# Attention units of a decoder layer: by token tile of a head pair instead of by branch

## The chip, the cores and the metric

The kernel runs on one core of a Trainium2 chip. The metric is the device time of one execution in microseconds; the kernel before was run three times (median 1426.13, from 1425.64 to 1426.88). A separate, profiled execution took 1427.72 us; its trace covers a span of 1425.9 us from the first to the last instruction.

## The reference, cut to what matters

One decoder layer on 256 tokens of width 2048, all in float32. After a norm, one matrix `w_in` projects to queries, keys, values and gates of two groups of 16 heads of 64. The first 16 heads are "NSA" heads: four query heads share a key/value head, and each head mixes three branches. With 256 tokens all four blocks of 64 keys are selected and the window of 512 covers everything, so the selected and the window branch are both plain causal attention over all keys, with the same relative bias, but with keys and values of their own:

```python
s = einsum(q, k_slc) * scale + bias        # 256 x 256, causal, per head
o_slc = masked_softmax(s) @ v_slc
s = einsum(q, k_win) * scale + bias_w      # the same bias by distance
o_win = masked_softmax(s) @ v_win
o = g0 * o_cmp + g1 * o_slc + g2 * o_win   # gates per token and head
```

The third branch attends to 15 compressed blocks. The other 16 heads ("FoX") are causal attention with a forget gate. Both are normed, multiplied by `w_out` and added to the input; then come a router and 32 experts (top two), whose weights alone are some 400 MB, and a last norm.

## The kernel before, in words

The work has three stages. In the first (to about 370 us of the span) `w_in` streams through SBUF in 44 items; each item is four chunks of 12 matmuls that accumulate into PSUM. Float32 accuracy comes from splitting each operand x into hi + lo, two numbers in the faster float32r form, and adding the products hi·hi, hi·lo and lo·hi: `stream_conv` makes the two halves of a weight (ACT writes hi at L187, DVE writes lo at L188) into one of three buffers, two half items ahead. In the second stage `w_out` streams in the same way (`wo`, 386 to 460 us). The third is the experts: their weights stream through a ring of SBUF slots (`expert_load`, L960); a load is issued by SP when its slot is free and when the stage allows it (`ring["ready"]`, `ring["used"]`, both advanced as the matmuls are issued).

The order on every engine is the order of the program. Attention is woven into the streaming: after every chunk `background()` advances the pipeline `attn_pipe` by one step. Its four steps per unit are: `a` of the next unit, `b` of the unit before it, nothing, `c` of the unit before it. One unit is thus consumed per item; there are 16 units for the NSA heads and 8 for FoX.

An NSA unit (class `Unit`) is one branch `br` of a pair of heads (pair `p`, 8 pairs):

- `a` computes logits of both heads, for the token tile t=1 (tokens 128 to 255, 256 keys) and t=0 (128 keys), into one PSUM bank per head; DVE adds the bias and takes the row maximum (L573), ACT takes the exponential and its sum (L575), DVE inverts the sum, multiplies by the gate and scales (L579 to L584).
- `b` turns the probabilities round by six 128x128 transposes (L591 to L593) and copies them out of PSUM, head 0 on DVE, head 1 on ACT (L595).
- `c` multiplies with the values: four products, head 0 into rows 0 to 63 of the bank `o` and head 1 into rows 64 to 127. At the pair's second branch the compressed branch is added (`pTc`) and ACT copies the result out (L614).

The logits use the same split. `split_k` writes for each key head hi and lo, each in both halves of the partitions; `split_q` writes a head's q as hi in one half and lo in the other (`qs`). The two products of a head are

```python
(qs[:, j, h, tk], kk[:, 0, g, keys])      # 128 rows: hi and lo of q with hi of k
(qs[hp, j, h, tk], kk[hp, 1, g, keys])    # 64 rows: hi of q with lo of k
```

where `hp` is rows 0 to 63 for head 0 and rows 64 to 127 for head 1. `mm` (L114) issues all of these matmuls, so in the profile they are told apart by the names of their tiles: `s_n` logits, `t_n` transposes, `o` values (`_f` for FoX).

Of the kernel before, what the change touches and what calls it, by code (L numbers as in the profile page):

```python
# [80 lines left out]
def tile_kernel(ctx: ExitStack, tc: tile.TileContext, a: dict, out):  # L81
# [441 lines left out]
    kT, vN = {}, {}  # L523

    def split_k(tmp, kk):
        for gp in range(2):
            hp, op_ = slice(64 * gp, 64 * gp + 64), slice(64 - 64 * gp, 128 - 64 * gp)
            act.copy(kk[hp, 0, gp::2, :], tmp[hp])
            dve.tensor_tensor(kk[hp, 1, gp::2, :], tmp[hp], kk[hp, 0, gp::2, :].bitcast(F32), ALU.subtract)
            yield  # L530
            for part in range(2):
                act.copy(kk[op_, part, gp::2, :], kk[hp, part, gp::2, :].bitcast(F32))
                yield

    def post_kv(b, br):
# [4 lines left out]
        splits.append(split_k(tmp, kk))  # L540
# [3 lines left out]
        kT[br], vN[br] = kk, vt  # L544


    sq = fp.tile([P, 2, T], F32, name="sq")

    class Unit:
# [3 lines left out]
        def __init__(self, name, qk, bias, v, gmul, first, last, pair):  # L553
            self.__dict__.update(locals())

        def a(self):
# [21 lines left out]
            for h in range(2):  # L578
                dve.tensor_scalar(sm[:, h], sm[:, h], 1e-30, None, ALU.max)  # L579
                dve.reciprocal(sm[:, h], sm[:, h])  # L580
                if self.gmul is not None:
                    dve.tensor_tensor(sm[:, h], sm[:, h], self.gmul[:, h], ALU.mult)
# [3 lines left out]
        def b(self):  # L586
            self.t = []
            for h in range(2):
# [5 lines left out]
                pT = wk.tile([P, 384], F32, tag="pT", name=f"pT_{self.name}_{h}", bufs=4)  # L594
                (act.copy if h else dve.tensor_copy)(pT, tp[:, 0:384])  # L595
                self.t.append(pT)

        def c(self):
            pr = self.pair
            if self.first:  # L600
                pr["o"] = bank(f"o{pr['i']}", "o")
            oT = pr["o"]
            hp = [slice(0, 64), slice(64, 128)]
            nsa = pr["i"] < 8
            for h in range(2):
                mm(oT[hp[h], 0:T], self.v[h][0], self.t[h][:, 0:T], self.first, False)
            for h in range(2):
                mm(oT[hp[h], P:T], self.v[h][1], self.t[h][:, T:T + P], False, self.last and not nsa)
            if self.last:
                i = pr["i"]  # L610
                if nsa:
                    G, j = divmod(i, 4)
                    mm(oT[:, :T], vcbd[0][:, G, j, :], pTc[G], False, True)
                act.copy(oraw[i // 8][:, i % 8, :], oT[:, :T])  # L614
                part = i // 8
                if i % 8 == 0:
                    pool.tensor_tensor(sq[:, part, :], oraw[i // 8][:, i % 8, :], oraw[i // 8][:, i % 8, :], ALU.mult)
                else:
                    s2 = wk.tile([P, T], F32, tag="pcm", name=f"s2_{i}", bufs=1)
                    pool.tensor_tensor(s2, oraw[i // 8][:, i % 8, :], oraw[i // 8][:, i % 8, :], ALU.mult)  # L620
                    pool.tensor_tensor(sq[:, part, :], sq[:, part, :], s2, ALU.add)
# [71 lines left out]
    def post_q(b, G):  # L693
# [7 lines left out]
        for j in range(4):  # L701
# [5 lines left out]
            def bias_of(g=g, hs=hs, nxt=j % 2 == 1):  # L707
                bi = nsa_bias(g)
                if nxt:
                    nsa_bias(g + 1) if g < 3 else fox_bias(0)  # L710
                return [(bi[:, hh, P - 1::-1], bi[:, hh, T - 1::-1]) for hh in hs]

            for br in range(2):
                def qk(h, t, keys, j=j, g=g, kk=kT[br]):
                    tk, hp = slice(t * P, (t + 1) * P), slice(64 * h, 64 * h + 64)
                    return [(qs[:, j, h, tk], kk[:, 0, g, keys]), (qs[hp, j, h, tk], kk[hp, 1, g, keys])]

                units.append(Unit(f"n{p}{br}", qk, bias_of,
                                  [[vN[br][:, t, 64 * g:64 * g + 64] for t in range(2)]] * 2,
                                  gb[:, 2 * p:2 * p + 2, :, br + 1], br == 0, br == 1, pair))  # L720
# [15 lines left out]
    def post_fkv(b, G, hf):  # L736
# [5 lines left out]
        for j in range(2):  # L742
# [10 lines left out]
            def qk(h, t, keys, j=j):  # L753
# [6 lines left out]
                              None, True, True, pair))  # L760
# [728 lines left out]
```

## Time and profile before

| | |
|---|---|
| median of 3 runs | 1426.13 us |
| profiled execution | 1427.72 us, span 1425.9 us |
| TensorE busy | 1321.7 us, 93% of the span |
| DVE, ACT, POOL busy | 509.2, 315.3, 75.9 us |
| HBM read | 476.63 MB |
| attention units of the NSA heads | 125 to 278 us of the span |

A busy TensorE says that an instruction was in it, not that it streamed columns: matmuls overlap, and a gap of a tenth of a microsecond between two starts is counted as busy. What an instruction costs is therefore read here from the distance between starts on the time line, not from its duration. In a row of a time line, the number before the engine is the time from the first start to the last end of the group, and a shape such as 64*128 is rows times columns of the stationary operand.

### The profile page before, as it was taken

The page shows a single profiled execution, that of the slowest core. Times are in us where ns is not written, and L with a number is a line of the kernel's source. Part 1 is how long each engine was busy: PE and PEld are TensorE (multiplying, and loading weights), DVE is VectorE, ACT ScalarE, POOL GpSimd, SP SyncE. Part 2 cuts the span into 40 slices and gives each one's busy share as a digit, 9 for nine tenths or more (in the row PEclk, how much of TensorE's full clock was granted, in tenths as well). Part 3 has the DMA queues.
Part 4 walks back from the last instruction along what each step waited for, and adds up shares of the span by engine and source line. Part 5 has one row for each costly group of instructions (what it writes and reads, how often), then busy time and mean ns, then how long its engine had stood idle before and what let it go on. Part 6 is the DMA issues. An engine that isn't in the chain of part 4 may idle for free.

```text
span 1425.9 us, 18327 instructions
## 1 busy us (share of the span) xinstructions
PE 1321.7 (93%) x7526; PEld 771.5 (54%) x7526; DVE 509.2 (36%) x1046; ACT 315.3 (22%) x632; POOL 75.9 (5%) x94
## 2 busy tenths in 40 slices
PE   9999999999999899999998997997998899799885
PEld 8999999889787534334333432433433344243332
DVE  4656877766756304114113021220401212031022
ACT  5455555545545100100100000000000000000003
POOL 0300010131100003000000000000000000000003
PEclk9999999999999999999999999999999999999998
DMA  8654454555595999999999999999999999999994
GB/s 270 211 165 149 133 143 134 182 171 167 197 378 184 362 398 422 399 421 421 421 421 421 421 420 421 421 420 421 421 420 421 421 421 421 421 420 421 421 405 162
DMA packets 116698, 480.04 MB, mean 337 GB/s; under 512 B 14368, under 2 KB 40832, under 8 KB 68352
## 3 DMA queue, kind: packets, MB, share of 16 engines
q1 hardware_dynamic: 112240, 474.53, 84.5%
q10 hardware_dynamic: 4368, 4.27, 0.9%
q8 instruction: 61, 1.00, 0.3%
q14 instruction: 29, 0.24, 0.1%
HBM read 476.63 MB, written 2.14 MB: 336 GB/s over the span
## 4 chain that ended last, share of the span: by engine, by line
PE 56%; DMA 37%; DVE 4%; ACT 2%; issue 1%; SPq 0%; ACTq 0%; POOL 0%; DVEq 0%; POOLq 0%
DMA e_u<-in_expert_w_up_dram 17%; DMA e_d<-in_expert_w_down_dram 17%; PE bu L114 12%; PE fkv_ps L114 6%; PE wo L114 6%; PE bg L114 4%; PE by L114 4%; PE bo L114 3%; PE q_ps L114 3%; PE fq_ps L114 3%; PE bx L114 3%; DMA e_g<-in_expert_w_gate_dram 3%; PE kcv_ps L114 2%; PE o L114 2%; PE kvw_ps L114 2%; PE kvs_ps L114 2%
## 5 line engine op out<-in xcount | busy, mean ns | idle before, releaser
L114 PE MATMUL by<-e_d,hids 128*64 128x512 f32 (+2 forms) x1072 | 234.0, 576 | 32.5 <-DMA e_d<-in_expert_w_down_dram 31.8
L114 PE MATMUL bu<-e_u,xg 128*64 128x512 f32 x1024 | 243.9, 597 | 9.7 <-DMA e_u<-in_expert_w_up_dram 9.6
L114 PE MATMUL bg<-e_g,xg 128*64 128x512 f32 x1024 | 234.8, 596 | 12.9 <-DMA e_g<-in_expert_w_gate_dram 12.9
L1273 DVE TENSOR_TENSOR ys<-by,ys 128x512 fp32r<-128x512 f32 x60 | 40.0, 687 | 454.1 <-ACT ys L1272 452.8
L114 PEld LDWEIGHTS by<-e_d,hids 128*64 128x64 f32 x1072 | 77.4, 137 | 181.8 <-issue 122.1
L114 PEld LDWEIGHTS bg<-e_g,xg 128*64 128x64 f32 x1024 | 81.7, 137 | 143.2 <-issue 107.0
L114 PEld LDWEIGHTS bu<-e_u,xg 128*64 128x64 f32 x1024 | 75.6, 136 | 148.3 <-issue 121.5
L1287 DVE TENSOR_TENSOR y<-y,bo 128x512 f32<-128x512 f32 x112 | 72.0, 684 | 152.7 <-PE bo L114 152.7
L1272 ACT CAST ys<-by 128x512 fp32r<-128x512 f32 x60 | 35.2, 586 | 311.8 <-PE by L114 197.2
L114 PE MATMUL bo<-ys,scT 128*128 128x512 f32 x240 | 73.5, 426 | 13.4 <-DVE y L1287 5.8
L114 PE MATMUL wo<-cv_wo,ohi 128*128 128x512 f32 x256 | 80.6, 396 | 0.0
L114 PEld LDWEIGHTS bx<-s,hh 128*128 128x128 f32 x512 | 62.2, 188 | 23.8 <-issue 13.0
L114 PE MATMUL bx<-s,hh 128*128 128x256 f32 x512 | 68.7, 287 | 4.6 <-DVE y L1287 2.9
L114 PEld LDWEIGHTS bo<-ys,scT 128*128 128x128 f32 x240 | 38.0, 188 | 60.1 <-issue 44.3
L1201 DVE TENSOR_TENSOR xg<-bx,fw 128x512 f32<-128x512 f32 x64 | 43.5, 690 | 75.3 <-PE bx L114 75.3
L114 PE MATMUL fkv_ps<-xhl,cv_fkv 128*128 128x256 f32 x384 | 59.7, 291 | 0.0
L114 PE MATMUL fkv_ps<-cv_fkv,xhl 128*128 128x256 f32 x384 | 56.3, 282 | 0.0
L1395 POOL TENSOR_TENSOR o<-y,e_fnw 128x256 f32<-128x256 f32 (+2 forms) x12 | 10.1, 866 | 835.9 <-DVE y L1308 835.9
L188 DVE TENSOR_TENSOR cv_fkv<-raw_fkv,cv_fkv 128x1024 fp32r<-128x1024 f32 x32 | 43.1, 1348 | 28.5 <-ACT cv_fkv L187 28.4
L114 PEld LDWEIGHTS wo<-cv_wo,ohi 128*128 128x128 f32 x256 | 46.9, 188 | 10.4 <-issue 1.2
L114 PE MATMUL fq_ps<-xhl,cv_fq 128*128 128x256 f32 x384 | 52.4, 289 | 0.0
L114 PEld LDWEIGHTS fkv_ps<-xhl,cv_fkv 128*128 128x128 f32 x384 | 50.3, 190 | 2.2 <-issue 1.2
(285 smaller groups left out, 1439.4 us busy)
## 6 DMA issues: line engine op xcount, KB each, us to landing
e_g<-in_expert_w_gate_dram SPq DMA_DIRECT2D x128, 1024.0 KB, 19.8
e_u<-in_expert_w_up_dram SPq DMA_DIRECT2D x128, 1024.0 KB, 19.8
e_d<-in_expert_w_down_dram SPq DMA_DIRECT2D x124, 1024.0 KB, 19.8
raw_fkv<-in_w_in_dram SPq DMA_DIRECT2D x32, 512.0 KB, 4.9
raw_wo<-in_w_out_dram SPq DMA_DIRECT2D x16, 1024.0 KB, 5.2
raw_q<-in_w_in_dram SPq DMA_DIRECT2D x8, 1024.0 KB, 5.2
raw_fq<-in_w_in_dram SPq DMA_DIRECT2D x8, 1024.0 KB, 5.1
raw_kvs<-in_w_in_dram SPq DMA_DIRECT2D x4, 1024.0 KB, 6.4
```

The costliest lines, as they stand in the source:

```text
L114: pe.matmul(o, l, r, start=start, stop=stop, skip_group_check=True)
L188: dve.tensor_tensor(lo, r, hi.bitcast(F32), ALU.subtract)
L1201: dve.tensor_tensor(xt_[:, i0:i0 + per, 0:m], bx.rearrange("p (i s) -> p i s", i=per), fw[:, 4 * j + i0:4 * j + i0 + per].unsqueeze(2).bro ...
L1272: act.copy(hi, by[n])
L1273: dve.tensor_tensor(lo, by[n], hi.bitcast(F32), ALU.subtract)
L1287: dve.tensor_tensor(y[t][:, ns], base[t][:, ns], bo, ALU.add)
L1395: (dve if last else pool).tensor_tensor(o[t][:, ns], y[t][:, ns], fnw[:, ns], ALU.mult)
```

## The change

A unit is now a token tile t of a head pair with both branches (class `Tile`); t=1 goes first, then t=0. Keys of both branches lie side by side in two tiles, `kp[0]` (hi, in both halves of the partitions) and `kp[1]` (lo in rows 0 to 63, zeros in rows 64 to 127, written once by POOL). A head's q is hi in rows 0 to 63 and lo in rows 64 to 127, for both heads alike. A head's logits are two products over 128 rows whose moving operand holds both branches: 512 columns for t=1, 256 for t=0. The t=0 logits of both heads share one bank. The sums of both heads and branches are inverted and gated together. `b` does eight transposes for t=1 and four for t=0; the latter are copied out in one piece by ACT. `c` runs for t=0 only, with eight value products and the compressed branch. The 16 units stay 16; FoX units compute what they did. `kc2` (keys and values of the compressed branch) moves to the two buffers of the bias, since `m0` now holds `kp[1]` from the start.

```diff
     def post_kcv(b):
-        t_ = m8("m0", "kc2", (2, 4, T))
-        kc2.extend(t_[:, i] for i in range(2))
+        kc2.extend(ap_q.tile([P, 4, T], F32, tag="m6", name=f"kc2{i}", bufs=2) for i in range(2))
...
-    def split_k(tmp, kk):
+    def split_k(tmp, br):
+        khi, klo = (k[:, :, br, :] for k in kp)
         for gp in range(2):
             hp, op_ = slice(64 * gp, 64 * gp + 64), slice(64 - 64 * gp, 128 - 64 * gp)
-            act.copy(kk[hp, 0, gp::2, :], tmp[hp])
-            dve.tensor_tensor(kk[hp, 1, gp::2, :], tmp[hp], kk[hp, 0, gp::2, :].bitcast(F32), ALU.subtract)
+            act.copy(khi[hp, gp::2, :], tmp[hp])
+            dve.tensor_tensor(klo[0:64, gp::2, :], tmp[hp], khi[hp, gp::2, :].bitcast(F32), ALU.subtract)
             yield
-            for part in range(2):
-                act.copy(kk[op_, part, gp::2, :], kk[hp, part, gp::2, :].bitcast(F32))
-                yield
+            act.copy(khi[op_, gp::2, :], khi[hp, gp::2, :].bitcast(F32))
+            yield
 
     def post_kv(b, br):
-
-        kk = m8(f"m{1 - br}", f"kT{br}", (2, 4, T), F32R)
+        if not kp:
+            kp.extend(m8(f"m{1 - i}", f"kT{i}", (4, 2, T), F32R) for i in range(2))
+            pool.memset(kp[1][64:128].bitcast(F32), 0.0)
...
+    class Tile:
...
+        def a(self):
+            name, t, g = self.name, self.t, self.g
+            bias = self.bias()
+            n = P + t * P
...
+            b = [bank(f"s_{name}_{i}", "s") for i in range(1 + t)]
+            sps = [b[t * h][:, (1 - t) * T * h:(1 - t) * T * h + 2 * n] for h in range(2)]
+            for h in range(2):
+                for i in range(2):
+                    mm(sps[h].rearrange("p (b k) -> p b k", b=2), self.q[:, h, t * P:(t + 1) * P],
+                       kp[i][:, g, :, 0:n], i == 0 and (t == 1 or h == 0), i == 1)
+            self.p = [wk.tile([P, 2, n], F32, tag="pr", name=f"pr_{name}_{h}", bufs=4) for h in range(2)]
+            for h in range(2):
+                pr = self.p[h]
+                for r in range(2):
+                    dve.tensor_tensor_reduce(out=pr[:, r], in0=sps[h][:, r * n:(r + 1) * n], in1=bias[h], scale=-1.0,
+                                             scalar=3.0e38, op0=ALU.add, op1=ALU.min, accum_out=st[:, h, r:r + 1])
+                    act.activation(pr[:, r], pr[:, r], AF.Exp, bias=st[:, h, r:r + 1], scale=-1.0,
+                                   accum_out=sm[:, h, r:r + 1])
+            dve.tensor_scalar(sm, sm, 1e-30, None, ALU.max)
+            dve.reciprocal(sm, sm)
+            dve.tensor_tensor(sm, sm, self.gmul, ALU.mult)
+            for h in range(2):
+                for r in range(2):
+                    dve.tensor_scalar(self.p[h][:, r], self.p[h][:, r], sm[:, h, r:r + 1], None, ALU.mult)
+
+        def b(self):
+            t, pr = self.t, self.pair
+            if t:
+                pr["pT"] = wk.tile([P, 2, 2, 384], F32, tag="pT", name=f"pT_{self.name}")
+                for h in range(2):
...
+                    (act.copy if h else dve.tensor_copy)(pr["pT"][:, h, :, P:], tp.rearrange("p (r k) -> p r k", r=2))
+            else:
...
+                act.copy(pr["pT"][:, :, :, 0:P], tp.rearrange("p (h r k) -> p h r k", h=2, r=2))
+
+        def c(self):
+            if self.t:
+                return
...
+            for b in range(2):
+                v = [vN[b][:, t, 64 * g:64 * g + 64] for t in range(2)]
+                for h in range(2):
+                    mm(oT[64 * h:64 * h + 64, 0:T], v[0], pT[:, h, b, 0:T], b == 0, False)
+                for h in range(2):
+                    mm(oT[64 * h:64 * h + 64, P:T], v[1], pT[:, h, b, T:T + P], False, False)
+            pair_end(self.pair["i"], oT)
...
     def split_q(s_, qs, j):
-        for h in range(2):
-            hp, op_ = slice(64 * h, 64 * h + 64), slice(64 - 64 * h, 128 - 64 * h)
-            act.copy(qs[hp, j:j + 2, h, :], s_[hp, j:j + 2, :])
-            dve.tensor_tensor(qs[op_, j:j + 2, h, :], s_[hp, j:j + 2, :], qs[hp, j:j + 2, h, :].bitcast(F32),
-                              ALU.subtract)
+        act.copy(qs[0:64, j:j + 2, 0, :], s_[0:64, j:j + 2, :])
+        dve.tensor_tensor(qs[64:128, j:j + 2, 0, :], s_[0:64, j:j + 2, :], qs[0:64, j:j + 2, 0, :].bitcast(F32),
+                          ALU.subtract)
+        u = qs[64:128, j:j + 2, 1, :]
+        act.copy(u, s_[64:128, j:j + 2, :])
+        act.copy(qs[0:64, j:j + 2, 1, :], u.bitcast(F32))
+        dve.tensor_tensor(u, s_[64:128, j:j + 2, :], u.bitcast(F32), ALU.subtract)
...
-            for br in range(2):
...
+            for t in (1, 0):
...
+                units.append(Tile(f"n{p}{t}", t, qs[:, j], g, bias_of,
+                                  gate.rearrange("p t (h b) -> p t h b", b=3)[:, t, 2 * p:2 * p + 2, 1:3], pair))
```

On TensorE, the logits of the first branch of pair 4 stood like this before, between two streaming matmuls (`fkv_ps`); `kT_812` holds the keys, `q_1828` the queries, `s_n_0` and `s_n_1` are the heads:

```order
L114 MATMUL fkv_ps_2314<-cv_fkv_0_2201,xhl_116 128x256
L114 MATMUL s_n_0_2329<-kT_812,q_1828 128x256
L114 MATMUL s_n_1_2330<-kT_812,q_1828 128x256
L114 MATMUL s_n_0_2329<-kT_812,q_1828 128x256
L114 MATMUL s_n_1_2330<-kT_812,q_1828 128x256
L114 MATMUL s_n_0_2329<-kT_812,q_1828 128x128
L114 MATMUL s_n_1_2330<-kT_812,q_1828 128x128
L114 MATMUL s_n_0_2329<-kT_812,q_1828 128x128
L114 MATMUL s_n_1_2330<-kT_812,q_1828 128x128
L114 MATMUL fkv_ps_2313<-xhl_114,cv_fkv_0_2201 128x256
```

Of these eight, the third, fourth, seventh and eighth are over 64 rows. The second branch repeats the eight. In the change the tile t=1 of the same pair has four (`kT_813` is `kp[0]`, `kT_814` is `kp[1]`):

```order
L114 MATMUL fkv_ps_2237<-cv_fkv_0_2136,xhl_116 128x256
L114 MATMUL s_n_0_2252<-kT_813,q_1789 128x512
L114 MATMUL s_n_0_2252<-kT_814,q_1789 128x512
L114 MATMUL s_n_1_2253<-kT_813,q_1789 128x512
L114 MATMUL s_n_1_2253<-kT_814,q_1789 128x512
L114 MATMUL fkv_ps_2236<-xhl_114,cv_fkv_0_2136 128x256
```

and the tile t=0, one item later, has four of 256 columns:

```order
L114 MATMUL fkv_ps_2237<-cv_fkv_0_2233,xhl_116 128x256
L114 MATMUL s_n_0_2361<-kT_813,q_1789 128x256
L114 MATMUL s_n_0_2361<-kT_814,q_1789 128x256
L114 MATMUL s_n_0_2361<-kT_813,q_1789 128x256
L114 MATMUL s_n_0_2361<-kT_814,q_1789 128x256
L114 MATMUL fkv_ps_2236<-xhl_114,cv_fkv_0_2233 128x256
```

Sixteen logits products of a pair have become eight, all over 128 rows. The value products of a pair stood in two places on TensorE; the second, of pair 0 and its window branch, was this (the first had four like them, and no `pTc`):

```order
L114 MATMUL o_1604<-pT_n_0_1676,vN_1139 64x256
L114 MATMUL o_1604<-pT_n_1_1682,vN_1139 64x256
L114 MATMUL o_1604<-pT_n_0_1676,vN_1139 64x128
L114 MATMUL o_1604<-pT_n_1_1682,vN_1139 64x128
L114 MATMUL o_1604<-pTc_1687,scaled 128x256
```

and is now one place with all eight (a row with x2 is the two heads):

```order
L114 MATMUL o_1684<-pT_n_1545,vN_817 64x256 x2
L114 MATMUL o_1684<-pT_n_1545,vN_817 64x128 x2
L114 MATMUL o_1684<-pT_n_1545,vN_1139 64x256 x2
L114 MATMUL o_1684<-pT_n_1545,vN_1139 64x128 x2
L114 MATMUL o_1684<-pTc_1655,scaled 128x256
```

On DVE, behind the four bias rows of a unit, the sums (`sm`) and probabilities (`pr`) were treated head by head, followed by the copy out of PSUM (pair 4, first branch):

```order
L579 TENSOR_SCALAR sm_n_2328<-sm_n_2328 128x2
L580 RECIPROCAL sm_n_2328<-sm_n_2328 128x2
L582 TENSOR_TENSOR sm_n_2328<-sm_n_2328,gate 128x2
L584 TENSOR_SCALAR pr_n_0_2339<-pr_n_0_2339,sm_n_2328 128x256
L584 TENSOR_SCALAR pr_n_0_2339<-pr_n_0_2339,sm_n_2328 128x128
L579 TENSOR_SCALAR sm_n_2328<-sm_n_2328 128x2
L580 RECIPROCAL sm_n_2328<-sm_n_2328 128x2
L582 TENSOR_TENSOR sm_n_2328<-sm_n_2328,gate 128x2
L584 TENSOR_SCALAR pr_n_1_2344<-pr_n_1_2344,sm_n_2328 128x256
L584 TENSOR_SCALAR pr_n_1_2344<-pr_n_1_2344,sm_n_2328 128x128
L595 COPY pT_n_0_2375<-t_n_0_2371 128x384
```

and are now treated together, before the next weight conversions (pair 4, t=1):

```order
L645 TENSOR_SCALAR sm_n_2251<-sm_n_2251 128x4
L646 RECIPROCAL sm_n_2251<-sm_n_2251 128x4
L647 TENSOR_TENSOR sm_n_2251<-sm_n_2251,gate 128x4
L650 TENSOR_SCALAR pr_n_0_2258<-pr_n_0_2258,sm_n_2251 128x256 x2
L650 TENSOR_SCALAR pr_n_1_2259<-pr_n_1_2259,sm_n_2251 128x256 x2
L188 TENSOR_TENSOR cv_fkv_1_2293<-raw_fkv_2024,cv_fkv_1_2293 128x1024
L188 TENSOR_TENSOR cv_fkv_0_2344<-raw_fkv_2133,cv_fkv_0_2344 128x1024
```

The copy of the tile t=1 on DVE now stands behind the scaling of t=0, and that of t=0 is on ACT. SP's order is the same as before; POOL has one more row, the memset, ahead of its work for the compressed branch.

## Rows read from the trace of the kernel before

**Rows 1.** Busy by stage: stretch, us, PE, PEld, DVE, ACT, POOL, clock, DMA share, GB/s

```profile
158.00:264.00 106.00, 105.77 (x840) 95.16 (x839) 81.02 (x253) 53.52 (x136) 12.68 (x17) 1.00 0.44 131
...
604.00:1426.00 822.00, 732.07 (x3464) 300.02 (x3464) 160.78 (x259) 65.63 (x141) 10.86 (x13) 0.99 0.99 409
...
430.00:440.00 10.00, 10.00 (x52) 7.72 (x51) 7.68 (x9) 4.75 (x8) 0.00 (x0) 1.00 0.34 119
```

**Rows 2.** The chain that ended last, in order of time (start us, us, what)

```profile
312.59 18.90 PE fkv_ps L114 x156
...
387.99 35.49 PE wo L114 x156
...
602.34 0.84 PE bo L114 x3
603.18 19.83 DMA e_d<-in_expert_w_down_dram
```

**Rows 3.** Waits of TensorE, 120 to 310 us (us in total, times, longest)

```profile
PE o L114 <- DVE pT_n L595: 0.2, 1, 0.2
```

**Rows 4.** Time line of TensorE, one pair (start us, us, engine, line, names, count)

```profile
190.49 1.34 PE L114 MATMUL s_n<-kT,q 128*128 128x256 f32 x8
191.75 1.69 PE L114 MATMUL fq_ps<-xhl,cv_fq 128*128 128x256 f32 x12
193.28 0.27 PE L591 MATMUL t_n<-cst,pr_n 128*128 128x128 f32 x1
...
193.85 3.10 PE L114 MATMUL fq_ps<-xhl,cv_fq 128*128 128x256 f32 x24
196.89 0.87 PE L114 MATMUL o<-pT_n,vN 128*64 128x256 f32 x8
197.69 0.98 PE L114 MATMUL fkv_ps<-xhl,cv_fkv 128*128 128x256 f32 x6
...
199.22 1.34 PE L114 MATMUL s_n<-kT,q 128*128 128x256 f32 x8
...
205.62 0.87 PE L114 MATMUL o<-pT_n,vN 128*64 128x256 f32 x8
...
208.40 0.40 PE L114 MATMUL s_n<-kT,q 128*128 128x256 f32 x2
```

**Rows 5.** The same time line in narrow windows inside the unit at 190.49 us

```profile
190.37 0.28 PE L114 MATMUL fq_ps<-xhl,cv_fq 128*128 128x256 f32 x1
190.49 0.40 PE L114 MATMUL s_n<-kT,q 128*128 128x256 f32 x2
...
190.82 0.38 PE L114 MATMUL s_n<-kT,q 64*128 64x256 f32 x2
...
191.50 0.33 PE L114 MATMUL s_n<-kT,q 64*128 64x128 f32 x2
```

**Rows 6.** Time line of ACT and TensorE around the first unit

```profile
123.53 1.26 ACT L631 CAST q<-scaled 64x512 fp32r<-64x512 f32 x2 [1.89 <-DVE scaled L338]
...
125.64 1.32 PE L114 MATMUL s_n<-kT,q 128*128 128x256 f32 x7 [0.34 <-DVE q L632]
```

**Rows 7.** Time lines of DVE and ACT in the unit at 199.22 us

```profile
200.59 0.42 DVE L573 CUSTOM_DVE_ANT_0 pr_n<-s_n,bias 128x256 f32<-128x256 f32 x1 [0.84 <-PE s_n L114]
...
202.08 0.17 DVE L579 TENSOR_SCALAR sm_n<-sm_n 128x2 f32<-128x2 f32 x1 [0.29 <-ACT pr_n L575]
202.28 0.17 DVE L580 RECIPROCAL sm_n<-sm_n 128x2 f32<-128x2 f32 x1
...
204.20 0.55 DVE L595 COPY pT_n<-t_n 128x384 f32<-128x384 f32 x1
...
201.06 0.51 ACT L575 ACTIVATE pr_n<-pr_n,st_n 128x256 f32<-128x256 f32 x1 [2.95 <-DVE st_n L573]
...
201.57 0.39 ACT L575 ACTIVATE pr_n<-pr_n,st_n 128x128 f32<-128x128 f32 x1
```

**Rows 8.** DVE by line and shape, 158 to 300 us (busy us, mean ns | idle before)

```profile
L188 DVE TENSOR_TENSOR cv_fkv<-raw_fkv,cv_fkv 128x1024 fp32r<-128x1024 f32 x17 | 23.5, 1380 | 14.2 <-ACT cv_fkv L187 14.2
```

More of the change, by code (lines that the diff above doesn't have):

```diff
@@ L520, in compress @@
         yield
[L523 to L525 removed]
+    kp, vN = [], {}
+    def split_k(tmp, br):
+        khi, klo = (k[:, :, br, :] for k in kp)
         for gp in range(2):
             hp, op_ = slice(64 * gp, 64 * gp + 64), slice(64 - 64 * gp, 128 - 64 * gp)
[L528 to L529 removed]
+            act.copy(khi[hp, gp::2, :], tmp[hp])
+            dve.tensor_tensor(klo[0:64, gp::2, :], tmp[hp], khi[hp, gp::2, :].bitcast(F32), ALU.subtract)
             yield
[L531 to L533 removed]
+            act.copy(khi[op_, gp::2, :], khi[hp, gp::2, :].bitcast(F32))
+            yield
     def post_kv(b, br):
[L537 removed]
+        if not kp:
+            kp.extend(m8(f"m{1 - i}", f"kT{i}", (4, 2, T), F32R) for i in range(2))
+            pool.memset(kp[1][64:128].bitcast(F32), 0.0)
         tmp = scaled[:, 0:2, :]
         row_scale(tmp, b[0].rearrange("p (c t) -> p c t", c=2))
[L540 removed]
+        splits.append(split_k(tmp, br))
         vt = fp.tile([P, 2, T], F32, name=f"vN{br}")
@@ L543, in post_kv, with pair_end, __init__ @@
             act.activation(vt[:, t, :], b[1][:, t * 256:t * 256 + 256], AF.Copy, scale=rsx[:, t:t + 1])
-        kT[br], vN[br] = kk, vt
+        vN[br] = vt
     sq = fp.tile([P, 2, T], F32, name="sq")
+    def pair_end(i, oT):
+        if i < 8:
+            G, j = divmod(i, 4)
+            mm(oT[:, :T], vcbd[0][:, G, j, :], pTc[G], False, True)
+        act.copy(oraw[i // 8][:, i % 8, :], oT[:, :T])
+        part = i // 8
+        if i % 8 == 0:
+            pool.tensor_tensor(sq[:, part, :], oraw[i // 8][:, i % 8, :], oraw[i // 8][:, i % 8, :], ALU.mult)
+        else:
+            s2 = wk.tile([P, T], F32, tag="pcm", name=f"s2_{i}", bufs=1)
+            pool.tensor_tensor(s2, oraw[i // 8][:, i % 8, :], oraw[i // 8][:, i % 8, :], ALU.mult)
+            pool.tensor_tensor(sq[:, part, :], sq[:, part, :], s2, ALU.add)
     class Unit:
-        def __init__(self, name, qk, bias, v, gmul, first, last, pair):
+        def __init__(self, name, qk, bias, v, pair):
             self.__dict__.update(locals())
@@ L593, in b @@
                 pe.transpose(tp[:, 0:P], pr[:, 2 * P:3 * P], ident)
-                pT = wk.tile([P, 384], F32, tag="pT", name=f"pT_{self.name}_{h}", bufs=4)
-                (act.copy if h else dve.tensor_copy)(pT, tp[:, 0:384])
-                self.t.append(pT)
+                (act.copy if h else dve.tensor_copy)(self.t[:, h], tp[:, 0:384])
         def c(self):
[L599 to L602, printed above, removed]
@@ L603, in c @@
-            hp = [slice(0, 64), slice(64, 128)]
-            nsa = pr["i"] < 8
+            i = self.pair["i"]
+            oT = bank(f"o{i}", "o")
             for h in range(2):
-                mm(oT[hp[h], 0:T], self.v[h][0], self.t[h][:, 0:T], self.first, False)
+                mm(oT[64 * h:64 * h + 64, 0:T], self.v[h][0], self.t[:, h, 0:T], True, False)
             for h in range(2):
[L608 to L621, printed above, removed]
@@ L705, in post_q, with bias_of @@
             hs = [2 * (j % 2), 2 * (j % 2) + 1]
[L707 to L711, printed above, removed]
-            for br in range(2):
[L714 to L720, printed above, removed]
+            for t in (1, 0):
+                def bias_of(t=t, g=g, hs=hs, nxt=j % 2 == 1):
+                    bi = nsa_bias(g)
+                    if nxt:
+                        nsa_bias(g + 1) if g < 3 else fox_bias(0)
+                    return [bi[:, hh, t * P + P - 1::-1] for hh in hs]
+                units.append(Tile(f"n{p}{t}", t, qs[:, j], g, bias_of,
+                                  gate.rearrange("p t (h b) -> p t h b", b=3)[:, t, 2 * p:2 * p + 2, 1:3], pair))
     def fox_bias(p):
@@ L759, in post_fkv @@
                                for h in range(2)],
-                              None, True, True, pair))
+                              pair))
     fmem = {}
```

21 lines of the change are left out of this document (18 added, 3 removed).

## The prediction

> **What bounds the kernel now.** I read three views in this order. First the busy time by stage: from 604 us on the DMA engines are 99% busy at 409 GB/s, so the experts' stage ends when their weights have come in. Between 158 and 264 us, where most NSA units lie, TensorE is busy for 105.77 of 106 us and DMA at 44% [rows 1]. Second the chain that ended last: streaming matmuls up to 602.34 us, and only then a DMA, released by TensorE, followed by one load after another [rows 2]. The loads cannot start earlier by themselves: at 430 to 440 us the DMA share is 0.34 [rows 1], since slots and the stage hold SP back, and both are given free by matmuls. So whatever TensorE saves in the first stage moves everything behind it, the end included. Third the waits: in the NSA units TensorE waits for almost nobody (0.2 us for the copied probabilities [rows 3], 0.34 us for the first queries [rows 6]). What it does not wait for it must be doing, so the question is what a unit costs on TensorE itself.
>
> That is read from the distance between starts. The pair from 190.49 to 208.40 us takes 17.91 us [rows 4]. In it are 96 streaming matmuls of 256 columns; undisturbed ones come every 18.90/156 = 0.121 us [rows 2], 11.63 us for 96. Left for attention: 6.28 us per pair.
>
> **Logits.** A branch takes 191.75 - 190.49 = 1.26 us, and the 12 streaming matmuls behind it 193.28 - 191.75 = 1.53 instead of 1.454: 1.34 us, or 2.67 per pair [rows 4]. The columns don't account for it. The narrow windows show why: the stream passes into the first 128-row product at the normal distance (190.37 to 190.49), and the two 128-row products of 256 columns are started within 0.12. Then nothing starts until 190.82, where the two 64-row products start together (two of them last 0.38, as one does) [rows 5]. By the usual distance they could have started at 190.73; the same kind of hole stands at each later passage between 64 and 128 rows. Columns alone would be 2 x 0.121 for the 128-row products, 0.121 for the 64-row ones side by side, and half of that again for t=0: 0.545 us. So some 0.79 us of a branch's 1.34 are holes.
>
> The change has no 64-row logits left. Its four products of 512 columns I price by the 128-row, 512-column matmuls of `wo`, 35.49/156 = 0.2275 us each, its four of 256 by the stream, 0.121 [rows 2]: 0.91 + 0.485 = 1.395 us per pair. Saved: 1.28 us. Not shown before is a moving operand in two runs of 128 (t=0). From below it costs nothing; from above it counts as two 128-column products, for which the nearest rows are the transposes, 0.57/6 = 0.095 each [rows 4]: 4 x (0.19 - 0.121) = 0.28 us per pair. I take nothing, since the nearest in bytes and columns is the stream.
>
> [...]
>
> **Values.** Four `o` products with their holes take 197.69 - 196.89 = 0.80 us; behind them 12 streaming matmuls take 199.22 - 197.69 = 1.53, 0.08 too much; ahead of them 24 take 196.89 - 193.85 = 3.04 against 2.91, of which I give half, 0.065, to the passage from the transposes [rows 4]. The change does all eight at once, so one such visit of 0.945 us goes and four products are added without the passages: I take 0.65 us, with 0.55 and 0.80 (the whole visit) as ends. Saved: 0.29 us per pair. The transposes stay twelve.
>
> **Sum.** 1.28 + 0.29 = 1.57 us per pair, 12.6 us for eight.
>
> **The first unit** is the one place where TensorE already waits for queries. Head 1's query now goes through one more ACT copy before DVE can subtract; a copy is 1.26/2 = 0.63 us [rows 6]. Head 0's two products can go at their old time, head 1's start at about 126.2 instead of all being under way at 125.64; that unit's saving is nearly eaten: 0.4 us back. The same copy at the other three splits has several items of lead, and two copies per branch are gone in `split_k`. Remaining: 12.2 us.
>
> **What is costed at nothing, and its cover.** The softmax chain. DVE begins 200.59 - 199.22 = 1.37 us after the first logit, ACT 0.47 later, and an exponential over 256 comes every 0.51 us [rows 7]. For t=1 four of those end at 1.37 + 0.47 + 2.04 = 3.9 us; t=0's copy of the pair before stands behind them on ACT and lands at about 4.5. Its reader, `c`, starts after the logits (0.91), three chunks (4.36) and four transposes (0.5), at 5.8: 1.3 us of cover. Before, the copy on DVE ended at 204.75 for an `o` at 205.62, 0.87 us [rows 4, 7], so the tightest reader gets looser. Waiting for all four sums before the first scaling makes DVE idle longer, but t=1's probabilities are wanted only five chunks later. DVE itself was busy 81.02 of 106 us [rows 1], 13.7 per pair; six small operations at 0.2 [rows 7] and about 0.4 of copies go: 12.1 of 16.3. POOL's memset comes once, on an engine that is busy 5% of the span, and SP's order is untouched. Bounds for all this: 0 to 0.5 us of waits per pair, 4 us in all.
>
> The profiled execution of 1427.72 us would become 1415.5; it stood 1.6 above the median, and from the median, 1426.13 - 12.2, I forecast **1413.9 us**.
>
> **Rivals.**
>
> *Part of it is eaten.* The chain is late in some units: those where the compressed branch's operations stand on DVE too, or where a conversion delays the logits' reader (DVE sat idle for 14.2 us before 17 conversions, waiting for ACT [rows 8]; a longer run of exponentials on ACT can push these). At 0.5 to 1.1 us per pair it gives 1417.5 to 1423, say 1420. Against it: cover of 1.3 us, and waits of 0.2 us so far.
>
> *The holes are not the rows'.* If they belong to the change of bank or of stationary operand, they stay, 0.79 x 2 per pair, and the lost side-by-side run adds 1.395 - 1.09 = 0.3 us, 2.4 in all; the value products' 2.3 us cancels it: 1426, no change. Against it: between the two heads bank and stationary operand change without a hole, and so they do from the stream [rows 5]. [...] The same time comes out if the change shortens the first stage and the experts' loads do not move; against that stands the chain.
>
> *Slower: a PSUM bank.* The logits, the transposes and the compressed branch share three banks. The copy of t=1, head 0, stands on DVE behind the whole of t=0 and may hold the bank that the next t=1 needs. By the rows it lands some 4.8 us after t=0's logits (0.5 to begin, 0.47, four exponentials at 0.39, sums 0.8, scaling 0.8, copy 0.7), and the next t=1 comes 7.1 after them (0.485, four chunks 5.8, eight transposes 0.8). From 7.1 on TensorE waits; from 8.7 the wait eats all 1.57. Three late conversions ahead of it (1.38 each [rows 8]) and a begin at 1.37 instead of 0.5 would bring it to 9.8: 2.7 us of wait, eight times 1.1 lost, 1435.
>
> **How the numbers follow.** Forecast 0.80; part eaten 0.10; no change 0.05; slower 0.05. The forecast's own range is 1411 (1.57 becomes 1.7 and the first unit loses nothing) to 1417.5 (0.28 of the two runs and some waits). With the nearer half of the second case the range is 1411 to 1419.5. A measurement of this kernel can tell about 0.2%, 2.9 us, from no change, so below 1423.3 is faster: 0.90; same 0.05; slower 0.05.
>
> **What would show it.** Right: the holes gone from the time line, 512-column `s_n` about 0.228 us apart, the four of t=0 about 0.121, logits of a pair near 1.4 us; one `o` visit per pair of some 1.45 us before `pTc`; a pair without extras near 16.3 us; the last NSA logits, the start of `wo` and the first DMA of the late chain all earlier by the same 12 us. Wrong: waits of `o` or `s_n` on ACT or DVE in the units, t=0 products further apart, or a late chain that has not moved.

## The result, and the profile after

The changed kernel takes 1417.93 us (median of 4, 1417.33 to 1419.14); the kernel before, measured beside it, 1426.51 (median of 4, 1425.64 to 1428.22). The ratio is 0.9939, interval 0.9922 to 0.9957: 8.6 us faster, where 12.2 were forecast (1413.9, range 1411.0 to 1419.5). The profiled execution took 1417.83 us with a span of 1416.1.

**A pair on TensorE.** The time line of one pair after the change, to be laid beside [rows 4] (columns as there):

```profile
188.76 0.64 PE L114 MATMUL s_n<-kT,q 128*128 128x256 f32 x4
189.24 1.60 PE L114 MATMUL fq_ps<-xhl,cv_fq 128*128 128x256 f32 x12
...
195.86 1.09 PE L114 MATMUL s_n<-kT,q 128*128 128x512 f32 x4
196.79 0.87 PE L114 MATMUL fkv_ps<-xhl,cv_fkv 128*128 128x256 f32 x6
...
201.62 1.52 PE L114 MATMUL o<-pT_n,vN 128*64 128x256 f32 x16
203.07 0.70 PE L114 MATMUL o<-pTc,scaled 128*128 128x256 f32 x2
...
205.04 0.40 PE L114 MATMUL s_n<-kT,q 128*128 128x256 f32 x2
```

From start to start: t=0's logits take 189.24 - 188.76 = 0.48 us, t=1's 196.79 - 195.86 = 0.93, the eight value products (float32, at most 256 columns, two rows each in the trace) 203.07 - 201.62 = 1.45, 0.18 each, where the stream's float32r products of 256 columns come every 18.90/156 = 0.121. The pair takes 205.04 - 188.76 = 16.28 us instead of 17.91: 1.63 saved where 1.57 was forecast. Eight such pairs would be 13.0 us.

**Stages.** The same stretches as in [rows 1], the second cut at the new end:

```profile
158.00:264.00 106.00, 104.08 (x858) 98.48 (x857) 79.47 (x240) 61.49 (x155) 12.79 (x17) 1.00 0.46 144
604.00:1416.00 812.00, 723.44 (x3424) 299.83 (x3424) 157.05 (x253) 65.06 (x140) 10.85 (x13) 0.99 0.99 409
```

The experts' loads run at the same 409 GB/s and simply start earlier. In the NSA stretch TensorE is no longer all busy: 1.92 us of 106 are idle, 0.23 before. The waits of TensorE from 120 to 310 us say on what, for the whole of the units; before the NSA units had 0.2 us [rows 3] beside the first unit's 0.34 [rows 6]:

```profile
PE bpt L741 <- DVE st_n L641: 2.8, 2, 1.9
PE csc L114 <- DVE st_n L641: 1.0, 1, 1.0
PE s_n L114 <- DVE q L695: 0.5, 1, 0.5
```

`csc` are the logits of the compressed branch, `bpt` the transposes of its probabilities. Both want a PSUM bank of the logits' three, and wait until DVE's bias rows (`st_n`) have read an earlier unit. The time lines of TensorE and DVE at the longest of them:

```profile
140.44 1.09 PE L114 MATMUL s_n<-kT,q 128*128 128x512 f32 x4
...
142.79 0.60 PE L667 MATMUL t_n<-cst,pr_n 128*128 128x128 f32 x4
145.26 0.41 PE L741 MATMUL bpt<-cst,pcm 128*128 128x128 f32 x2 [1.87 <-DVE st_n L641]
```

```profile
138.53 0.17 DVE L645 TENSOR_SCALAR sm_n<-sm_n 128x4 f32<-128x4 f32 x1 [1.09 <-ACT pr_n L643]
...
139.94 0.68 DVE L662 COPY pT_n<-t_n 128x512 f32<-128x512 f32 x1
140.54 0.39 DVE L730 TENSOR_REDUCE ss<-scs 128x16 f32<-128x240 f32 x1
...
141.75 0.41 DVE L735 TENSOR_TENSOR pcm<-scs,ss 128x240 f32<-128x240 f32 x1
142.08 2.35 DVE L188 TENSOR_TENSOR cv_q<-raw_q,cv_q 128x1024 fp32r<-128x1024 f32 x2
144.35 0.42 DVE L641 CUSTOM_DVE_ANT_0 pr_n<-s_n,bias 128x256 f32<-128x256 f32 x1
```

TensorE's last product of t=1's logits ends at 141.53, but DVE first does the compressed normalisation (140.54 to 142.08) and two conversions, and begins with the logits at 144.35, 2.8 us later. In the kernel before DVE went through the same operations and was *not* late:

```profile
141.87 2.35 DVE L188 TENSOR_TENSOR cv_q<-raw_q,cv_q 128x1024 fp32r<-128x1024 f32 x2
144.62 0.42 DVE L573 CUSTOM_DVE_ANT_0 pr_n<-s_n,bias 128x256 f32<-128x256 f32 x1 [0.40 <-PE s_n L114]
```

There DVE waited 0.40 us for TensorE; the slow logits were the cover. Two things took it away. Counted from each kernel's first logits (124.92 before, 124.01 after), TensorE comes to these logits 1.90 us earlier after the change (16.43 instead of 18.33 us), and DVE comes to the two conversions 1.12 us later (18.07 instead of 16.95). DVE is later by itself because the joint sums wait for four exponentials: 1.1 us in each unit, where the first head's sums waited 0.29 [rows 7]. For twelve units of the stretch after the change:

```profile
L645 DVE TENSOR_SCALAR sm_n<-sm_n 128x4 f32<-128x4 f32 x12 | 3.2, 265 | 13.2 <-ACT pr_n L643 13.2
```

**Behind the units.** The table gives the distances between first starts of named TensorE groups, read from the time lines, for both kernels and three runs of the next section:

| us | before | before + products (e12) | after | after + products (e6) | e9 |
|---|---|---|---|---|---|
| first `s_n` to first `s_f` (NSA units) | 146.30 | 146.29 | 137.04 | 137.05 | 134.49 |
| first `s_f` to first `wo` (FoX units) | 88.42 | 86.67 | 87.40 | 87.26 | 86.46 |
| first `wo` to first `bx` | 112.42 | 112.40 | 112.42 | 112.43 | 112.41 |
| first `bx` to first `bsc` (experts' start) | 22.49 | 22.41 | 23.84 | 22.50 | 22.48 |
| first `bsc` to last `bo` | 916.02 | 916.45 | 916.08 | 916.58 | 915.98 |

The first row repeats to 0.01 us in two kernels with the same units, so where TensorE's granted clock holds (1.00 from 158 to 264 us before and after; in e5, below, 0.66 from 163 to 173 us) a difference there is the change's: 9.26 us. It counts 0.43 us too many, since after the change the whole value visit of the last pair stands behind the first `s_f`, and the second row is longer by that. Up to the second `s_f` the units take 155.16 us before and 146.33 after: 8.83 us saved. In the fourth row 1.35 us is given back. The chain that ended last shows it at its third row here; before the same 32 products took 4.17:

```profile
301.41 18.90 PE fkv_ps L114 x156
...
376.80 35.49 PE wo L114 x156
...
460.87 5.57 PE bx L114 x32
...
593.01 20.26 DMA e_d<-in_expert_w_down_dram
```

The first two answer to [rows 2] with the same durations, both 11.2 us earlier, 0.91 of which stand ahead of the units (124.92 to 124.01); the late chain's first DMA went from 603.18 to 593.01. Windows on the router's end and the products behind it, before, after and e6 (columns as in [rows 1]; the eighth figure is the granted clock):

```profile
467.20:473.20 6.00, 2.48 (x22) 2.20 (x22) 5.54 (x31) 0.42 (x2) 0.73 (x1) 1.00 1.02 426
473.20:477.20 4.00, 4.00 (x31) 3.25 (x31) 2.77 (x4) 0.00 (x0) 0.00 (x0) 1.00 1.02 422
```

```profile
456.00:462.00 6.00, 2.48 (x20) 2.20 (x19) 5.55 (x31) 0.42 (x2) 0.73 (x1) 0.93 1.01 425
462.00:466.00 4.00, 4.00 (x26) 4.00 (x25) 1.85 (x3) 0.00 (x0) 0.00 (x0) 0.68 1.01 424
```

```profile
455.70:461.70 6.00, 5.24 (x47) 4.88 (x46) 5.58 (x31) 0.42 (x2) 0.76 (x1) 1.00 1.01 426
461.70:465.70 4.00, 4.00 (x32) 3.25 (x32) 2.77 (x4) 0.00 (x0) 0.00 (x0) 1.00 1.01 426
```

In both kernels TensorE is busy for 2.48 of 6 us there. After it the clock of the changed kernel stands at 0.68 of full speed in the mean (0.50 from 462 to 464 us), in the profiled execution of before at 1.00. With added products TensorE is busy for 5.24 us and the clock stays at 1.00.

### The profile page after: what moved, and what is told of

Read it like the earlier page. It is cut to its first block, busy times and chain, and to the rows that moved or that the text cites. A ratio compares the mean times of both kernels' runs of the same rounds, so it can differ in the third digit from the quotient of the medians.

```text
span 1416.1 us, 18174 instructions
## 1 busy us (share of the span) xinstructions
PE 1310.2 (93%) x7462; PEld 769.4 (54%) x7462; DVE 496.6 (35%) x990; ACT 316.3 (22%) x632; POOL 79.7 (6%) x95
## 4 chain that ended last, share of the span: by engine, by line
PE 50%; DMA 42%; DVE 4%; ACT 2%; issue 1%; POOL 0%; SPq 0%; DVEq 0%; ACTq 0%; POOLq 0%
DMA e_u<-in_expert_w_up_dram 16%; DMA e_d<-in_expert_w_down_dram 16%; DMA e_g<-in_expert_w_gate_dram 11%; PE bu L114 7%; PE fkv_ps L114 6%; PE wo L114 6%; PE bg L114 5%; PE by L114 5%; PE fq_ps L114 3%; PE bx L114 2%; PE q_ps L114 2%; PE bo L114 2%; PE kcv_ps L114 2%; PE kvw_ps L114 2%; PE kvs_ps L114 2%; PE o L114 2%
## 5 line engine op out<-in xcount | busy, mean ns | idle before, releaser
L114 PEld LDWEIGHTS bu<-e_u,xg 128*64 128x64 f32 x1024 | 78.6, 136 | 143.5 <-issue 114.3
```

What stands on the lines that cost most here:

```text
L114: pe.matmul(o, l, r, start=start, stop=stop, skip_group_check=True)
```

## The experiments

**e1: is it the PSUM bank or DVE?**

```diff
+        if G:
+            yield
         csc = bank(f"csc{G}", "s")
...
-        bpt = bank(f"bpt{G}", "s")
+        bpt = bank(f"bpt{G}", "o")
```

> The change, with the compressed branch's transposes (bpt) in the bank of the value products instead of one of the three shared logits banks, and the second group's compressed logits (csc) one pipeline step later. Theory A (a shared bank that DVE has not yet read holds TensorE: bpt 2.8 us in two waits, csc 1.0 us in one): these waits go, the last NSA logits come 3.8 us earlier than with the change, and the time falls from 1417.9 to about 1414. Theory B (DVE is simply late there, whatever the bank): the waits move to the next reader, the time falls by less than 1 us.

1419.71 us (median of 5, ratio to before 0.9949, 0.9936 to 0.9963). The waits changed their name only, 4.9 us instead of 3.8:

```profile
PE o L114 <- ACT pTc L745: 3.2, 2, 2.0
PE o L114 <- ACT pT_n L668: 1.7, 1, 1.7
```

Another bank lets `bpt` start, but ACT's copies then stand behind exponentials whose bias rows are just as late. The bank was where the lateness was seen, not where it came from.

**e2: are the holes those of the 64-row products?** In `Tile.a`, the second product of each head over half the rows:

```diff
+                    rows = slice(0, 64 if i else P)
-                    mm(..., self.q[:, h, ...], kp[i][:, g, :, 0:n], ...)
+                    mm(..., self.q[rows, h, ...], kp[i][rows, g, :, 0:n], ...)
```

> The change, but each head's second logits product contracts only the 64 rows that hold numbers (the zeros are left out); columns, banks and order are those of the change. Theory A (the holes come with the passage between 64 and 128 rows): every head's product gets a hole ahead (0.09 us) and behind (0.19), four times per pair, and two passages to the stream of 0.1: 1.3 us per pair, t=1 logits from 0.93 to about 1.5 us, in all 10.5 us slower than the change, about 1428. Theory B (the holes came with banks or stationary operands): nothing changes, 1418.

One run, 1424.63 us. Time line of a pair:

```profile
196.16 1.68 PE L114 MATMUL s_n<-kT,q 128*128 128x512 f32 x4
197.77 0.97 PE L114 MATMUL fkv_ps<-xhl,cv_fkv 128*128 128x256 f32 x6
...
206.12 1.22 PE L114 MATMUL s_n<-kT,q 128*128 128x256 f32 x4
207.26 0.98 PE L114 MATMUL fkv_ps<-xhl,cv_fkv 128*128 128x256 f32 x6
...
213.98 0.39 PE L114 MATMUL s_n<-kT,q 128*128 128x512 f32 x1
```

The same columns, half the rows in half the products, and t=1's logits take 1.61 us instead of 0.93, t=0's 1.14 instead of 0.48, the pair 17.82 instead of 16.28. Start by start, 0.09 us is lost at the first passage and 0.19 to 0.20 at each of the next three, into 64 rows as out of them, with 512 columns as with 256. So the holes belong to the passages between 128 and 64 rows. And there is no wait of `bpt` or `csc`: the slower TensorE is again DVE's cover.

**e3: the kernel before with 128 rows.** The second product then adds lo times lo as well.

```diff
-  return [(qs[:, j, h, tk], kk[:, 0, g, keys]), (qs[hp, j, h, tk], kk[hp, 1, g, keys])]
+  return [(qs[:, j, h, tk], kk[:, 0, g, keys]), (qs[:, j, h, tk], kk[:, 1, g, keys])]
```

> The kernel before, with its units by branch, in which the second logits product of a head contracts all 128 rows (hi and lo of q with lo of k; the term lo times lo is added, which is nearly zero) instead of 64. Theory A (holes): four products of 256 columns at 0.121 and four of 128 at 0.06 to 0.11 make 0.73 to 0.93 us instead of 1.34 per branch, 16 branches, 6.6 to 9.8 us faster than before: 1417 to 1420. It would give most of the logits' saving without the regrouping. Theory B (the side-by-side run was worth more than the holes cost): 0.18 us more per branch, 2.9 us slower, 1429.

1420.89 us (median of 4, 0.9958, 0.9943 to 0.9974). A branch's eight products take 196.99 - 196.12 = 0.87 us instead of 1.26:

```profile
196.12 1.04 PE L114 MATMUL s_n<-kT,q 128*128 128x256 f32 x8
196.99 0.93 PE L114 MATMUL fkv_ps<-xhl,cv_fkv 128*128 128x256 f32 x6
```

NSA units 141.66 us (first `s_n` to first `s_f`), 4.64 less than before, by rows alone. An undisturbed pair takes 17.09 us instead of 17.91, but the units have new waits here too: `o` and `t_n` wait 1.7 us for DVE. The other 0.81 us per pair come with the regrouping, with fewer products and one value visit.

**e4: value products in two visits.** `c` does the second branch; a new `c0`, one chunk earlier, the first:

```diff
+            if isinstance(prev, Tile):
+                prev.c0()
```

> The change, but the eight value products of a pair are issued in two visits (first branch one chunk earlier than the second), as before. Theory A (a visit costs its passages: 0.29 us, the term of the sum): a pair takes 16.56 instead of 16.27 us, 2.3 us in all, 1420. Theory B (passages cost nothing, the columns alone count): 16.27 us per pair, 1418.

One run, 1427.67 us. An undisturbed pair takes 16.61 us, 0.33 more: the second visit, as priced. The rest is not that price: `o` now waits 4.8 us for ACT's `pT_n`, `bpt` 2.2 for DVE, and the granted clock of the whole run was 0.988 (0.993 in the profiled run of the change), so the total says nothing of the visit.

**e5: the compressed branch ahead of the split of queries 2 and 3.**

```diff
-        misc.append(split_q_later(b, q, qs))
         misc.append(compressed(G, q))
+        misc.append(split_q_later(b, q, qs))
```

> The changed kernel with two lines exchanged: the compressed branch is put into the queue of small steps ahead of the split of queries 2 and 3, so that its operations begin one item earlier on DVE and the split comes behind them. Theory 'DVE is late where the compressed branch's operations meet the new t=1 chain': spread over other items, the waits of TensorE on DVE's st_n (bpt 2.8, csc 1.0 us in the changed kernel) fall to at most 1 us, the first wo comes up to 3 us earlier, 1415 to 1416 us. Rival 'the chain of four sums is itself too long, whatever stands beside it': the waits stay at 3 to 4 us, or move to the split's readers (s_n <- DVE q), 1417.5 to 1419.

1419.28 us (median of 6, from 1416.72 to 1423.75; 0.9940, 0.9927 to 0.9954), a miss in both theories. The profiled run is the slowest of the six. `bpt` waits no more, but `csc` of the second half comes before its own queries are scaled:

```profile
163.13 2.72 PE L114 MATMUL csc<-kcd,scaled 128*128 128x32 f32 x12 [1.99 <-DVE scaled L338]
165.66 2.91 PE L114 MATMUL fq_ps<-xhl,cv_fq 128*128 128x256 f32 x12
```

and behind the wait twelve streaming matmuls take 2.7 us to the next group (168.37) instead of 1.45, at a granted clock of 0.66 from 163 to 173 us. From this unit's logits to the next unit's it is 16.27 us; with the change it is 12.17, with a wait of `csc` of 1.0. So a wait of 2 us cost more than 2. The clock also fell in the first half, where `csc` waits for nothing (0.69 of full speed in the mean from 130 to 134 us). NSA units 139.45 us.

**e6: products that compute nothing in the router.**

```diff
-    keep_clock("clock1", 17)
+    keep_clock("clock1", 25)
...
     mm(brk[:, 32:64], lt, sel[:, 1, :], False, True)
+    keep_clock("clock2", 4)
```

> The changed kernel with matmuls that compute nothing in the router: clock1 has 25 products instead of 17, and four more (clock2) follow the third brk product, where TensorE was idle. Theory 'TensorE's granted clock falls to half behind the idle stretch in the router, and that gives back 1.3 us of the gain': bx x32 returns from 5.6 to about 4.2 us, the granted clock from 460 to 470 us is 1.0 again, and the late chain moves by 1.3 us more: about 1416.6. Rival 'the loads that wait on the stage's end do not depend on it': clock 1.0 but the end unchanged, 1418. If the added products stand in the way of the router's own: 1418.5.

1416.30 us (median of 5, 1415.47 to 1417.18; 0.9923, 0.9910 to 0.9936). The clock holds (1.00 in both windows above), `bx` to `bsc` is 22.50 us again, and it reaches the end: the slowest of these runs is faster than the fastest without the products (1417.33), though the intervals of the two ratios overlap.

**e7: e5 and e6 together.**

> Both edits, the exchanged lines and the products in the router. If the two effects are separate they add: 1414 to 1415 us, where the forecast was 1413.9. If the first moves the waits only: as e6, 1416.6.

1416.52 us (median of 6, 0.9927, 0.9914 to 0.9941): no more than e6 alone. `csc` still waits, 2.3 us; the twelve matmuls behind it take 1.75, and the NSA units 136.67.

**e8: no compressed softmax.** From `scs` to `pcm` all is left out but the memset.

> The changed kernel without the compressed branch's softmax: its bias, maximum, exponential and normalisation on DVE and ACT are left out (its logits, transposes and value products stay on TensorE, over zeros). Theory 'these operations make DVE late for the t=1 chain': bpt and csc wait for DVE under 0.5 us instead of 3.8, the first wo and the end come 3.5 to 4 us earlier, 1414. Rival 'the four sums' chain is too long by itself': at least 2 us of waits of bpt, csc or o stay, 1416 to 1418.

1416.74 us (median of 4, 0.9926, 0.9912 to 0.9941). The waits of TensorE, 120 to 310 us:

```profile
PE csc L114 <- DVE st_n L641: 1.0, 1, 1.0
...
```

`bpt`'s 2.8 us are gone, `csc`'s 1.0 stays; the NSA units take 133.82 us, 3.2 less. The total shows only 1.2 of it. In the profiled run `bx` to `bsc` takes 24.64 us, 0.8 more than with the change, and the granted clock of the whole run is 0.990 (0.993 with the change); whether that explains the median is not shown.

**e9: e6, with part of the compressed softmax on POOL.**

```diff
-        dve.tensor_scalar(mx, mx, -1e29, ...);  dve.tensor_tensor(scv, scv, mx...)
+        pool.tensor_scalar(mx, mx, -1e29, ...); pool.tensor_tensor(scv, scv, mx...)
-        dve.tensor_tensor(ss..., gate...);  dve.tensor_tensor(pcm..., scv, ss...)
+        pool.tensor_tensor(ss..., gate...); pool.tensor_tensor(pcm..., scv, ss...)
```

> The changed kernel with the products in the router (clock1 25, clock2 4) and four operations of the compressed softmax per half moved from DVE to POOL: the clamp of the maximum and the subtraction, the gate product and the last scaling (0.17 + 0.41 + 0.18 + 0.41 = 1.2 us of DVE each time). Theory 'DVE is late for the t=1 chain': DVE's bias rows begin about 1 us earlier, bpt's two waits fall from 2.8 to about 1 us in all, csc's 1.0 stays, the end comes 1 to 2 us earlier than with the products alone (1416.3): 1414.5 to 1415.5. Rival 'POOL's operations slow DVE beside them or are late themselves': waits of bpt on POOL's pcm or of ACT on POOL, 1416.5 to 1418.

1414.75 us (median of 5, from 1411.99, the profiled run, to 1415.61; 0.9911, 0.9898 to 0.9925). DVE and TensorE at the place shown above:

```profile
139.68 2.32 DVE L188 TENSOR_TENSOR cv_q<-raw_q,cv_q 128x1024 fp32r<-128x1024 f32 x2
141.93 0.41 DVE L641 CUSTOM_DVE_ANT_0 pr_n<-s_n,bias 128x256 f32<-128x256 f32 x1
```

```profile
141.81 0.60 PE L667 MATMUL t_n<-cst,pr_n 128*128 128x128 f32 x4
142.84 0.41 PE L741 MATMUL bpt<-cst,pcm 128*128 128x128 f32 x2 [0.43 <-DVE st_n L641]
```

The bias rows begin 0.1 us after the transposes ahead of `bpt`, not 1.6, and `bpt` waits 0.4 us in all.

**e10: e9, with `csc` of the second half one item later** (its `yield` as in e1).

> As the one before, with csc of the second half one item later, past the unit whose logits' banks it waits for. If its wait of 1.0 us was that of the bank alone, it goes: 1413.5 to 1414.5, and the first wo comes at least 13 us earlier than in the kernel before, counted from the first s_n. Rival: the compressed operations, now one item later, make bpt's reader late instead, and o waits for ACT's pTc; then as the one before or slower by up to 1 us.

1414.66 us (median of 5, 0.9913, 0.9899 to 0.9926), the same as e9. `csc` waits no more, but `o` waits 2.0 us for ACT's `pT_n`: the rival, though it had named another copy, `pTc`.

**e11: the sums of each head apart.**

```diff
-            dve.tensor_scalar(sm, sm, ...); dve.reciprocal(sm, sm); dve.tensor_tensor(sm, sm, self.gmul, ALU.mult)
             for h in range(2):
+                dve.tensor_scalar(sm[:, h], ...); dve.reciprocal(sm[:, h], ...); dve.tensor_tensor(sm[:, h], ..., self.gmul[:, h], ...)
```

> The changed kernel with the sums of a unit clamped, inverted and gated for each head apart (six small operations on DVE instead of three), as before the change. Theory 'what makes the t=1 chain late is how much stands on DVE in the compressed branch's items': DVE's idle time of 1.09 us before the first sum falls to about 0.3 and three operations of 0.17 us come more, so the waits of bpt and csc stay near 3.8 us, between 2.8 and 4: 1417 to 1418.5. Rival 'the joint normalisation, which waits for four exponentials, is the cause': the waits fall below 2 us and the first wo comes 2 us earlier: 1415 to 1416.

1417.28 us (median of 4, 0.9932, 0.9917 to 0.9947), in the first theory's range; the waits lie between the two:

```profile
PE bpt L741 <- DVE st_n L641: 1.5, 2, 1.3
PE csc L114 <- DVE st_n L641: 0.8, 1, 0.8
```

1.5 of the 3.8 us go, so the joint normalisation has a share. It did not reach the NSA units in the profiled run (137.05 us again); why is not shown.

**e12: the kernel before with e6's products.**

> The kernel before with the added products in the router (clock1 25, clock2 4) and nothing else. If the drop of the clock at the experts' start is chargeable to the change (it was not in the profiled execution of the kernel before): no gain, within 0.5 us of its 1426 to 1427.5. Rival 'before has the same drop in most executions, its profiled one was an exception': about 1.3 us faster in the median, as the changed kernel was.

1424.42 us (median of 11) against 1426.44 (15 runs of before beside it): 0.9986, 0.9977 to 0.9995. The rival holds: the kernel before gains from these products as the changed one does. That its profiled execution, at a granted clock of 1.00 in the router, was an exception follows from that; no trace of another execution shows it. The granted clock of whole runs points the same way: a median of 0.993 over the 15 runs of before, of 0.996 over the 11 of e12.

## Why the prediction was right, and where it fell short

The mechanism was right and the time came out in the range, but with some luck: 1417.93 lies outside the forecast's own 1411 to 1417.5 and inside 1411 to 1419.5 only by the part of the first rival's case that was counted in (its nearer half would reach 1420.3, not 1419.5).

*Logits.* Right. 1.41 us per pair measured, 1.395 forecast; the moving operand in two runs of 128 costs nothing (0.48 us for four). That the holes are those of the rows is shown by e2 from one side and e3 from the other: a branch with its 64-row products side by side takes 1.26 us [rows 4], with all products over 128 rows 0.87 (e3).

*Values.* Right. One visit of 1.45 us; a second one costs 0.33 (e4), 0.29 was forecast.

*The first unit.* Right. Head 1's products start at 125.25, 1.24 us after head 0's; forecast was 126.2 on the old base of 124.92, 1.28 after. From first `s_n` to first `csc` 4.94 us became 4.67: 0.27 us saved, where a t=1 unit saves 1.34 - 0.93 = 0.41 elsewhere. So the 0.4 us given back was too much; 0.14 was lost.

*What is costed at nothing, and its cover.* This is the step that failed. It took 0 of the 0 to 4 us that it bounded itself; measured are 3.8 us of waits in three places. They cost a little more than their length: without `bpt`'s 2.8 the units are 3.2 us shorter (e8). That leaves 13.0 - 3.2 - 1.0 = 8.8 of the units' saving, and up to the second `s_f` it is 8.83. The cover of 1.3 us was worked out in a steady unit and DVE's load as a mean per pair (12.1 of 16.3). The compressed branch's operations stand in two groups of some 1.6 us, among query splits and conversions, where DVE had as little as 0.40 us to spare before; TensorE now comes 1.9 us earlier there and DVE itself 1.1 us later. It is the first rival's mechanism, at the place which that rival named, and 1417.93 lies at the edge of its 1417.5 to 1423. e8 shows `bpt`'s 2.8 us to be theirs; e9, which moves about 0.6 us of each group, takes away 2.4 us of them; with a slower TensorE they are gone (e2). Part is the joint normalisation (1.5 of the 3.8 us, e11), which the step had let pass because t=1's probabilities are wanted only five chunks later: what is queued on DVE behind the wait is wanted sooner. `csc`'s 1.0 us stays without the compressed operations (e8), so it is not theirs. The time line of DVE ahead of it, after the change, shows another term that had been taken at nothing:

```profile
160.97 0.69 DVE L695 TENSOR_TENSOR q<-scaled,q 64x512 fp32r<-64x512 f32 x1 [0.61 <-ACT q L694]
...
163.43 0.42 DVE L641 CUSTOM_DVE_ANT_0 pr_n<-s_n,bias 128x256 f32<-128x256 f32 x1
```

DVE waits 0.61 us there for the extra copy of the second half's first queries, which the prediction gave several items of lead. It begins with the bias rows 4.45 us after the first logit (158.98); at the same place before it was 2.40 (161.38 to 163.78). No run takes the copy away, so its share is not shown.

*The slower rival, a PSUM bank.* Did not come: the logits `s_n` wait for no bank, only for `q` in the first unit. Where banks do hold TensorE up, another bank gained nothing (e1).

*The late chain.* Right: what the first stage saves reaches the end one for one, in every column of the table (fifth row within 0.6 us).

*The rest.* The profiled executions differ by 9.9 us, the medians by 8.6. Three things in before's profile were its own and not the kernel's. The clock at the experts' start, on which 1.35 us hang, is one (e12); with the products in both kernels the change is worth 1424.42 - 1416.30 = 8.1 us by the medians and 9.0 by the two ratios (0.9923 / 0.9986), each taken beside its own runs of before. The second is the start of the program: the first `s_n` comes at 124.92 us in before and at 123.50 in e12, whose code is the same up to there; the granted clock of the first 24 us is 0.86 in before, and 0.93 in after, where the first `s_n` comes at 124.01. The third is a wait in the FoX units: 88.42 us in before, 86.67 in e12, whose code is the same there. The wait, then the time line of DVE, then POOL, in before:

```profile
PE o L114 <- DVE pT_f L595: 1.4, 1, 1.4
```

```profile
300.22 0.55 DVE L584 TENSOR_SCALAR pr_f<-pr_f,sm_f 128x256 f32<-128x256 f32 x2
...
301.10 2.62 DVE L584 TENSOR_SCALAR pr_f<-pr_f,sm_f 128x256 f32<-128x256 f32 x2
```

```profile
301.07 1.29 POOL L729 TENSOR_TENSOR fb<-fb,csf 128x512 f32<-128x512 f32 x1 [3.73 <-DVE sm_f L580]
302.31 1.33 POOL L730 TENSOR_TENSOR fb<-fb,csf 128x512 f32<-128x512 f32 x1
```

The same scaling takes 0.55 us alone and 2.62 beside two POOL additions; in e12 DVE came to the first of these scalings 1.44 us earlier and POOL to its additions 0.53 earlier (300.54), so these met a conversion instead.

*What stays open.* Why the granted clock fell behind the router in after's profile (0.68 in the mean of 462 to 466 us) but not in before's (1.00 from 473.2 to 477.2), though TensorE was equally idle ahead of it in both (busy for 2.48 of 6 us). Whether `csc`'s wait of 1.0 us is that of the extra copy, and whether it can be removed without making another (e10 did not), was not shown.

## What to carry to other kernels

Cover is not a property of the engine that is covered: it is the distance to the engine that comes next, and making the bottleneck faster takes from it. Work it out at the place where the side engine is fullest, not at a typical one, and count every operation queued ahead of the one that frees the buffer. Where a wait is named after a buffer, ask who is late in freeing it before moving to another buffer.

The best version here is the changed kernel with four small operations on POOL and the router's added products (e9): 1414.75 us, 0.9911 of before; e10 is the same.

## What had not been expected of the hardware

- A wait can cost more than its length: behind 2 us of waiting and the `csc` products twelve streaming matmuls took 2.7 instead of 1.45 us (e5, granted clock 0.66 from 163 to 173 us). The clock also fell behind the idle stretch of the router, to 0.50 from 462 to 464 us after the change. What makes it fall was not shown.
- Twelve products of 128 columns that compute nothing are worth 1.6 us in one kernel and 2.0 in the other (medians of e6 and e12; the interval of the second is 0.7 to 3.3).
- Operations of POOL and DVE took longer beside each other: DVE's two scalings 2.62 us instead of 0.55 (1.42 and 1.29 us, beside two POOL additions of 1.29 and 1.33, before); on POOL the scaling of `pcm` 1.46 us beside DVE's conversions (e9) and 0.60 beside its bias rows (e10, second half). Why was not shown.
